# Where weights are split and which PSUM bank takes turned data: four edits to a two-layer trunk on one core

## The chip, the cores and the metric

One Trainium2 core runs the whole kernel. The metric is the device time of one execution in microseconds (us). TensorE is called PE, VectorE DVE, ScalarE ACT, GpSimd POOL. Each engine works through its own instruction order and waits for others by semaphores.

## The reference

The kernel computes a trunk of two layers over 256 latent tokens of width 1024 (with 256 context tokens that serve the first layer's keys and values). Layer 0 mixes by differential attention (six heads) and a Fourier part, layer 1 by a gated mixer (SGU). Each layer is followed by a product-key expert network (PEER) with 16384 experts, and a norm ends it. Everything is float32. Cut to the parts that the change touches:

```python
# layer 0: per head, probabilities from two softmaxes, then values
p = jax.nn.softmax(s, axis=-1)
a = p[:, :, 0] - lam * p[:, :, 1]
return jnp.einsum('bhqk,bkhe->bqhe', a.astype(v.dtype), v)
...
# layer 1: the gated mixer
z = jax.nn.gelu(h @ w_in + b_in)
u, v = jnp.split(z, 2, axis=-1)
v = rmsnorm(v, ng).reshape(B, L // CHUNK, CHUNK, SGU_GROUPS, SGU_GC)
s = jnp.einsum('gpq,bnqgc->bnpgc', ws, v) + bs.T[None, None, :, :, None]
return (u * s.reshape(B, L, SGU_W)) @ w_out
...
x = x + g1 * y
x = x + g2 * peer_mix(rmsnorm(x, norm2_g[i]) * (1 + sc2) + sh2, ...)
```

The gates g1, g2 and the scales come from one vector per layer (`c_s @ ada_w[i] + ada_b[i]`), which the kernel gathers in the background.

## The kernel before

**Split weights.** A float32 product is made of three faster ones: a weight tile `raw` (128 x 1024, half a megabyte, one column block of the output) is split into `whi` (rounded, by ACT, L108) and `wlo` (the rest, by DVE, L110), and an activation in the same way (`thi`/`tlo`, `mhi`/`mlo`, `m1hi`/`m1lo`). `lin` (L240) issues whi by hi, whi by lo, wlo by hi. `S.next()` hands out the next split weight and `S.ahead()` splits one more, if a buffer is free; where it stands in the program is where ACT and DVE do that work, since the kernel's order is written out by hand and nothing is moved afterwards.

**PSUM.** There are eight banks of 128 x 512 in three pools: `mm` (2), `gg` (2) and `acc` (4), handed out by `mmb()`, `gb()` and `accb()`. A new user of a bank waits until the old one's readers are done. `gg` serves sums of squares (L263), spreads of a factor over the partitions (L276), the rope's permutation (L709), and the gates' sum `Ada.cols` (L459).

**Mixer 0.** A loop over heads runs by the table HEADS. `scores_parts` (L723) writes four `acc` banks, DVE takes maxima (L725), ACT exponentials (L733); `blend` (L747) makes `aa`; `turn` transposes it by PE (L755) into two banks, which ACT copies to `aT` (L756); `values` (L763) multiplies. The table TAIL does the last heads, the Fourier part (L908, L912, L916) and the gates (`A`, which calls `ada.cols()`), and begins the output columns d=0 and 1 (`w`). Then the loop over d (L949) makes the other columns; `residual` (L496) adds each to `x` and, from d=2 on, splits the next weight.

**The seam into mixer 1.** After PEER 0, `tail` transposes the sum back (L1219) and adds it to x, two columns d in one bank. `Norm.products` then starts the mixer's products before the norm's factor is known: columns 0 and 1, the sum of squares (ACT squares, DVE adds into `acc`, L306; `total`, L263), column 2, `factor` (L276, after POOL's power on `ir`, L268) and so on. In this norm (`lag`) the squares are taken at j = 1.

**Mixer 1** runs by the table SGU. V0 to V7 are half products for v (L247 to L249), E adds the bias and takes the gelu (z, L1280, then ACT's vv and vn), r and m scale v (vn, L1294), U6, U7, G6 and G7 make the last of u. Then for each group k of 128: p multiplies by the spatial weights (PE, L1308), x makes s (DVE, L1314), m = s u (DVE, L1318) and m1hi (ACT, L1319), l makes m1lo (DVE, L1324), and w0k, w1k, w2k add it to three output columns (PE, L240) at once. S is `S.ahead()` and N opens the next norm. Columns 3 to 7 follow in a loop over d.

Of the kernel before, what the change touches and what calls it, by code (L numbers as in the profile page):

```python
# [53 lines left out]
TAIL = "F0 s0 s1 s2 F1 s3 F2 F3 s4 fc u3 S t4 A n3 d0 d1 b N S v4 c1 u4 t5 c0 w00 v5 w11 w12 u5 n4 w06 w01 w03 n5 w13 S w04 w07 w16 w14 w05 w02 w15 w10 w17".split()  # L54

N1 = 3
SGU = "V0 S V1 S R E0 E1 V2 S V3 S E2 E3 V4 S V5 S E4 E5 V6 S V7 S E6 E7 r m0 m1 U6 S G6 U7 S G7 N p0 x0 p1 x1 l0 p2 x2 l1 p3 x3 l2 w00 w10 w20 p4 x4 l3 w01 w11 w21 p5 x5 l4 w02 w12 w22 p6 x6 l5 w03 w13 w23 p7 x7 l6 w04 w14 w24 l7 S w05 w15 w25 w06 w16 w26 w07 w17 w27".split()
START = "Lc Lx M0 sc M1 M2 M3 M4 M5 sx ic ix b S M6 S rc nc2 nc1 nc0 rx nc6 nx1 nx2 nc3 M7 nx0 nx3 C0 S nx4 M8 S Dc0 M9 S Dx0 Q000 M10 nx5 S Q010 M11 nc4 M12 Q020 nx7 S nc5 M13 Q030 M14 nc7 M15 nx6 C1 Q100 S Lk Q110 Dx1 Dc1 a Q120 S Q021 Q130 Q121 Q001 S Q101 Q111 a S Q031 a a Q011 V0 Q131 a Q220 S Q200 a a Q230 Q210 Q221 a S Q201 V1 a S Q231 S Q211 a V2".split()
HEADS = "k sum a turn ks a S score a q a rk a kc qs exp blend a values rq sc norm a S".split()
ADA_AT = list(range(68, 116, 6)) + list(range(132, 190, 4)) + list(range(190, 256, 2))  # L60
# [102 lines left out]
def trunk(ctx, tc, a, out):  # L163
# [8 lines left out]
    def mmb():  # L172
        return ps.tile([P, 512], F32, name="mm", bufs=2)

    def gb():
        return ps.tile([P, 512], F32, name="gg", bufs=2)

    def accb():
        return ps.tile([P, 512], F32, name="acc", bufs=4)

    S = Stream(nc, raws, hls)
    seen = set()
    for s in START:
        if s[0] == "M":
            n = int(s[1:])
# [48 lines left out]
    def lin(p, unit, xhi, xlo, order=range(KT), first=True, last=True, n=T, passes=(0, 1, 2)):  # L234
        (whi, wlo), o = unit, p[:, :n]
        terms = (whi, xhi), (whi, xlo), (wlo, xhi)
        for j, k in enumerate(order):
            for i in passes:
                w, t = terms[i]
                nc.tensor.matmul(o, lhsT=w[:, k, :], rhs=t[:, k, :n], start=first and j == 0 and i == passes[0],  # L240
                                 stop=last and j == len(order) - 1 and i == passes[-1])
# [38 lines left out]
    class Norm:  # L280
# [33 lines left out]
        def products(self, n, evict):  # L314

            self.lows(KT)
            p, u, t = [], [], []
            S.held = 2
            for j in range(n):
                p.append(accb() if j < 4 else mmb())  # L320
                u.append(S.next())
                if 0 < j < n - 1:
                    S.ahead()
                if j == 1:
                    for k in range(KT if self.lag else 0):
                        self.square(k)
                    for k, i in ([(k, i) for k in range(KT) for i in range(2)] if self.lag else
                                 [(k, i) for i in range(2) for k in range(KT - 1)] + [(KT - 1, 0), (KT - 1, 1)]):
                        lin(p[i], u[i], thi, tlo, (k,), n=W, passes=(0, 2), first=k == 0, last=False)
                    if not self.lag:  # L330
                        self.total()
                    for i in range(2):
                        lin(p[i], u[i], thi, tlo, n=W, passes=(1,), first=False)
                    S.held = 1
                elif j > 1:
                    lin(p[j], u[j], thi, tlo, n=W)
                if j == 2 and self.lag:
                    self.total()
                if j == (3 if self.lag else 1):
                    self.factor()  # L340
                    t = [self.scaled(k) for k in range(4)]
                if j == 1:
                    S.ahead()
            t += [self.scaled(k) for k in range(4, 6)]
            early = 2 if self.lag else 0
            for i in range(early):
                self.evict(p, i, evict)
            for k in range(KT):
                sh = self.shift[:, k:k + 1]
                A_.activation(thi[:, k, :T], t[k], AF.Identity, bias=sh)  # L350
                V.scalar_tensor_tensor(tlo[:, k, :T], t[k], sh, thi[:, k, :T].bitcast(F32),  # L351
                                       op0=OP.add, op1=OP.subtract)
                if k + 6 < KT:
                    t.append(self.scaled(k + 6))
                if k == 4:
                    S.ahead()
            return lambda: [self.evict(p, i, evict) for i in range(early, n)]
# [136 lines left out]
    def residual(nrm, d, p, gate, ahead=False):  # L494
        def add():
            V.scalar_tensor_tensor(x[:, d, :], p, gate, x[:, d, :], op0=OP.mult, op1=OP.add)  # L496
        if ahead:
            S.ahead(add)
        else:
            add()  # L500
        nrm.feed(d)


    with ExitStack() as mx:
# [14 lines left out]
        with tc.tile_pool(name="m0n", bufs=2) as npl:  # L519
# [101 lines left out]
            for s in START:  # L621
                c, n = s[0], s[1:]
# [10 lines left out]
                elif c == "M":  # L633
                    n = int(n)
# [22 lines left out]
                elif c == "D":  # L657
                    h, j = int(n[1]), n[0]
# [91 lines left out]
        def turn(h):  # L750
            aT = tmp.tile([P, 4, T], F32, name="aT", bufs=1)
            for qt, aa in enumerate(ea.pop(h)):
                p = accb()
                for k in range(4):
                    nc.tensor.transpose(p[:, k * P:(k + 1) * P], aa[:, k * P:(k + 1) * P], ident)  # L755
                A_.activation(aT[:, :, qt * P:(qt + 1) * P], p.rearrange("p (k q) -> p k q", k=4), AF.Copy)  # L756
            av[h] = aT
# [108 lines left out]
        def tail_step(s):  # L866
# [13 lines left out]
            elif c == "t":  # L880
                assert isinstance(ea[n], list)
                turn(n)
            elif c == "v":
                values(n)
# [62 lines left out]
            tail_step(s)  # L947
        assert "N" in have
        S.held = 1  # L949
        for d in range(8):  # L950
            if d < 2:
                p, u = first[d]
            else:
                p = mmb()
                lin(p, S.next(), mhi, mlo)
            residual(nrm, d, p[:, :T], mod[:, 0, 16 + d:17 + d], d > 1)

    def peer(layer, nrm, ln, last):


        with ExitStack() as px:
# [111 lines left out]
            r = routing()  # L1073
            with tc.tile_pool(name="rq", bufs=2) as rq:
                for half in range(2):
# [5 lines left out]
                    for l in range(0 if half else LATE, 8):  # L1081
                        p = mmb()
# [9 lines left out]
                    for tt in range(2):  # L1092
                        for g in range(2):
                            p = accb()
# [4 lines left out]
                            l0 = half * 8 + g * 4  # L1099
# [45 lines left out]
            def y_mult(i, halves=range(2)):  # L1145

                w = thi[:, i % 8, :T], tlo[:, i % 8, :T]
                e = [u.rearrange("p k c -> p (k c)") for u in units[i]]
                for n, (a_, b_) in enumerate(((0, 0), (1, 0), (0, 1))):
                    for tt in range(2):  # L1150
                        for h in halves:
                            nc.tensor.matmul(y[2 * h + tt], lhsT=w[a_][:, tt * P:tt * P + P],  # L1152
                                             rhs=e[b_][:, 512 * h:512 * h + 512],
                                             start=i == 0 and n == 0, stop=i == 127 and n == 2)

            g0 = gphase(0)
            for i in range(128):
# [6 lines left out]
                p = accb() if i < 120 else mmb()  # L1164
# [35 lines left out]
            def tail(ys):  # L1200

                ys = [t.rearrange("p (t c) -> p t c", t=2) for t in ys]
                for h in range(2):
                    if h == 0:
                        for i in range(128 - last, 128):
                            y_mult(i, (0,))
                    else:
                        y_mult(127, (1,))
                    A_.activation(ys[h][:, 0], y[2 * h], AF.Copy)
                    V.tensor_copy(ys[h][:, 1], y[2 * h + 1])  # L1210
                    if h == 0:
                        for i in range(128 - last, 127):
                            y_mult(i, (1,))
                    for d in range(4 * h, 4 * h + 4):
                        if d % 2 == 0:
                            p = mmb()
                        q = p[:, d % 2 * T:d % 2 * T + T]
                        for tt in range(2):
                            nc.tensor.transpose(q[:, tt * P:tt * P + P], ys[h][:, tt, d % 4 * P:d % 4 * P + P], ident)  # L1219
                        yield d, q, mod[:, layer, 40 + d:41 + d]  # L1220
# [7 lines left out]
    with mixer1 as mx:  # L1228
# [111 lines left out]

        for s in SGU:
            step1(s)
        assert "N" in have and wdone == [8] * N1
        S.held = 1
        for d in range(8):
            if d < N1:
                p = first[d][0]
            else:
                p = mmb()
# [127 lines left out]
```

## Time and profile before

| what | us |
| --- | --- |
| median of 3 runs | 1989.8 |
| lowest, highest | 1985.33, 1990.18 |
| the profiled execution's own time | 1987.19 |
| its span on the core | 1985.0 |
| PE busy in it | 1930.5 |
| DVE busy in it | 1567.0 |
| ACT busy in it | 935.9 |

Times in the rows below count from the start of the span. In the timeline a row merges instructions of one kind that follow one another; the number behind the x says how many. The idle time ahead of an instruction and who ended it stand in brackets. PE's idle time over the whole span is 54.5 us. The granted clock of PE is 1.00 (2.4 GHz) or 0.50 (1.2 GHz); its mean was 0.992.

### The profile page before, as it was taken

What the parts mean: (1) busy time and instruction counts of PE and PEld (TensorE: products, weight loads), DVE (VectorE), ACT (ScalarE), POOL (GpSimd) and SP (SyncE); (2) the same over time, 40 slices, a digit from 0 to 9 for tenths busy, and PEclk for the clock granted to TensorE, in tenths of its full rate; (3) what the DMA queues carried; (4) which work ended last, traced back from release to release, by engine and by line L of the source; (5) the groups of instructions that cost most, each with busy time, mean ns of one, the idle gap of its engine ahead of it and who ended that gap; (6) DMA issues with size and microseconds to landing.
All of it is one profiled execution on the core that took longest, in us unless ns stands there. A gap on an engine that the chain in (4) does not pass through costs nothing. (4 is left out here: it accounts for less than half of the span.)

```text
span 1985.0 us, 35614 instructions
## 1 busy us (share of the span) xinstructions
PE 1930.5 (97%) x14176; PEld 1726.4 (87%) x14176; DVE 1567.0 (79%) x2978; ACT 935.9 (47%) x1489; POOL 11.1 (1%) x17
## 2 busy tenths in 40 slices
PE   7999999999999999999998899999999999999997
PEld 3977999999999877788888899999999977778885
DVE  5786789987887899998887778997777788885554
ACT  5445554454444444444446554445444444444443
POOL 0000000000000000000000000000000000000000
PEclk8999999999999999999999999999999999999998
DMA  7742556656665566688885455555555555556662
GB/s 267 268 165 72 170 170 184 188 175 199 190 191 180 185 209 197 202 260 280 282 285 173 137 183 171 188 184 181 170 167 164 170 165 173 162 180 186 187 189 74
DMA packets 106150, 373.50 MB, mean 188 GB/s; under 512 B 11904, under 2 KB 12544, under 8 KB 105600
## 3 DMA queue, kind: packets, MB, share of 16 engines
q1 hardware_dynamic: 104256, 366.23, 57.6%
q10 hardware_dynamic: 1728, 5.00, 0.8%
q8 instruction: 111, 1.82, 0.4%
q14 instruction: 55, 0.45, 0.1%
HBM read 370.14 MB, written 1.05 MB: 187 GB/s over the span
## 5 line engine op out<-in xcount | busy, mean ns | idle before, releaser
L110 DVE TENSOR_TENSOR wlo<-raw,whi 128x1024 fp32r<-128x1024 f32 x604 | 737.3, 1223 | 225.1 <-ACT whi L108 217.1
L108 ACT ACTIVATE whi<-raw 128x1024 fp32r<-128x1024 f32 x604 | 635.5, 1055 | 418.2 <-PE acc L1152 328.1
L240 PE MATMUL acc<-thi,whi 128*128 128x256 f32 (+1 forms) x2016 | 571.1, 284 | 0.0
L240 PE MATMUL acc<-thi,wlo 128*128 128x256 f32 (+1 forms) x2016 | 567.7, 282 | 0.4 <-DVE wlo L110 0.4
L240 PE MATMUL acc<-tlo,whi 128*128 128x256 f32 (+1 forms) x2016 | 560.0, 281 | 0.0
L240 PEld LDWEIGHTS acc<-thi,wlo 128*128 128x128 f32 x2016 | 381.9, 189 | 1.0 <-DVE wlo L110 0.8
L240 PEld LDWEIGHTS acc<-thi,whi 128*128 128x128 f32 x2016 | 381.1, 189 | 0.0
L240 PEld LDWEIGHTS acc<-tlo,whi 128*128 128x128 f32 x2016 | 376.4, 188 | 0.0
L1152 PE MATMUL acc<-whi,thi 128*128 128x512 f32 x1024 | 285.6, 400 | 0.0
L1152 PE MATMUL acc<-whi,tlo 128*128 128x512 f32 x1024 | 281.3, 396 | 0.0
L1152 PE MATMUL acc<-wlo,thi 128*128 128x512 f32 x1024 | 281.1, 395 | 0.0
L1173 ACT ACTIVATE A<-acc 128x256 f32<-128x256 f32 x240 | 92.5, 386 | 394.0 <-PE acc L240 394.0
L1152 PEld LDWEIGHTS acc<-wlo,thi 128*128 128x128 f32 x1024 | 192.6, 188 | 47.5
L1152 PEld LDWEIGHTS acc<-whi,tlo 128*128 128x128 f32 x1024 | 192.6, 188 | 44.9
L1152 PEld LDWEIGHTS acc<-whi,thi 128*128 128x128 f32 x1024 | 187.2, 188 | 39.3
L1138 DVE SCALAR_TENSOR_TENSOR A<-gg,A 128x512 f32<-128x512 f32 x128 | 88.4, 690 | 74.8 <-PE gg L1135 74.8
L240 PE MATMUL mm<-thi,whi 128*128 128x256 f32 (+1 forms) x448 | 128.6, 287 | 0.9 <-ACT qp L1089 0.9
L240 PE MATMUL mm<-tlo,whi 128*128 128x256 f32 (+1 forms) x448 | 127.0, 284 | 2.4 <-DVE tlo L351 2.4
L240 PE MATMUL mm<-thi,wlo 128*128 128x256 f32 (+1 forms) x448 | 126.4, 282 | 0.0
L492 DVE TENSOR_TENSOR tlo<-A,thi 128x256 fp32r<-128x256 f32 x256 | 107.3, 420 | 0.0
L491 ACT ACTIVATE thi<-A 128x256 fp32r<-128x256 f32 x256 | 102.5, 401 | 0.0
L1135 PEld LDWEIGHTS <-o 128*128 128x128 f16 x2048 | 69.7, 97 | 31.3 <-DVE og L1124 13.5
(265 smaller groups left out, 2013.3 us busy)
## 6 DMA issues: line engine op xcount, KB each, us to landing
raw<-in_eu SPq DMA_DIRECT2D x256, 512.0 KB, 3.6
raw<-in_ev SPq DMA_DIRECT2D x256, 512.0 KB, 4.2
raw<-in_ada1t SPq DMA_DIRECT2D x56, 512.0 KB, 4.5
raw<-in_wq SPq DMA_DIRECT2D x32, 512.0 KB, 4.2
ada<-in_ada0t SPq DMA_DIRECT2D x48, 256.0 KB, 5.1
raw<-in_ada0h SPq DMA_DIRECT2D x16, 512.0 KB, 4.8
raw<-in_w_out SPq DMA_DIRECT2D x16, 512.0 KB, 3.7
raw<-in_o_in_u SPq DMA_DIRECT2D x8, 512.0 KB, 5.1
```

What stands on the lines that cost most here:

```text
L108: nc.scalar.activation(hi, r, AF.Copy)
L110: nc.vector.tensor_tensor(lo, r, hi.bitcast(F32), op=OP.subtract)
L240: nc.tensor.matmul(o, lhsT=w[:, k, :], rhs=t[:, k, :n], start=first and j == 0 and i == passes[0], stop=last and j == len(order) - 1 and i ...
L491: A_.activation(hi, src, AF.Copy)
L492: V.tensor_tensor(lo, src, hi.bitcast(F32), op=OP.subtract)
L1135: nc.tensor.matmul(pt[:, t, :], lhsT=o2[:, t // 2, :, t % 2], rhs=og[j][:, t // 2, :, t % 2], start=j == 0, stop=j == 1)
L1138: V.scalar_tensor_tensor(av, pt.rearrange("p t i -> p i t"), 1.0 / GSCALE, av, op0=OP.mult, op1=OP.mult)
L1152: nc.tensor.matmul(y[2 * h + tt], lhsT=w[a_][:, tt * P:tt * P + P], rhs=e[b_][:, 512 * h:512 * h + 512], start=i == 0 and n == 0, stop=i = ...
L1173: A_.activation(A[i // 64][:, i % 64, :], p[:, :T], AF.Gelu_apprx_tanh)
```

## The change

It has four parts. (1) `turn` takes its two banks from `gg`, not `acc`. (2) One more `S.ahead()` stands ahead of mixer 0's loop over d. (3) At the seam into mixer 1 the squares stand ahead of the splits, and `tail` takes every second bank from `gg`. (4) The table SGU has its S in other places.

```diff
-SGU = "V0 S V1 S R E0 E1 V2 S V3 S E2 E3 V4 S V5 S E4 E5 V6 S V7 S E6 E7 r m0 m1 U6 S G6 U7 S G7 N p0 x0 p1 x1 l0 p2 x2 l1 p3 x3 l2 w00 w10 w20 p4 x4 l3 w01 w11 w21 p5 x5 l4 w02 w12 w22 p6 x6 l5 w03 w13 w23 p7 x7 l6 w04 w14 w24 l7 S w05 w15 w25 w06 w16 w26 w07 w17 w27".split()
+SGU = "V0 S V1 S R E0 E1 V2 S S V3 S E2 E3 V4 S S V5 S E4 E5 V6 S V7 E6 E7 r m0 m1 U6 U7 G6 G7 p0 x0 p1 x1 l0 p2 x2 l1 p3 x3 l2 w00 w10 w20 p4 x4 l3 w01 w11 w21 N p5 x5 l4 S w02 w12 w22 p6 x6 l5 w03 w13 w23 p7 x7 l6 S w04 w14 w24 l7 w05 w15 w25 w06 w16 w26 w07 w17 w27 S".split()
...
-                if 0 < j < n - 1:
+                if 0 < j < n - 1 and not (self.lag and j == 1):
                     S.ahead()
                 if j == 1:
                     for k in range(KT if self.lag else 0):
                         self.square(k)
+                    if self.lag:
+                        S.ahead()
...
             for qt, aa in enumerate(ea.pop(h)):
-                p = accb()
+                p = gb()
...
         S.held = 1
+        S.ahead()
         for d in range(8):
...
                         if d % 2 == 0:
-                            p = mmb()
+                            p = gb() if d % 4 else mmb()
```

Three places show how it moves the instructions. A row is one engine's instruction (or several alike) in program order: line, operation, output and inputs, shape. The change's lines are 2 to 3 higher than the same lines before.

**PE in mixer 0's tail.** `ones` and `osq` are a head's sum of squares, `ident` and `aa` the transposes of `turn` for head 4, `blocks` and `fold` the gates' sum. Before:

```order
L263 MATMUL acc<-ones,osq 128x1 x2
L755 MATMUL acc<-ident,aa 128x128 x8
L459 MATMUL gg<-blocks,fold 128x24 x4
L276 MATMUL acc<-ident,ir 128x128 x2
L908 MATMUL mm<-cst,ft 128x512 x4
L763 MATMUL acc<-aT,vt 128x256 x4
```

With the change:

```order
L263 MATMUL acc<-ones,osq 128x1 x2
L757 MATMUL gg<-ident,aa 128x128 x8
L461 MATMUL gg<-blocks,fold 128x24 x4
L276 MATMUL acc<-ident,ir 128x128 x2
L910 MATMUL mm<-cst,ft 128x512 x4
L765 MATMUL acc<-aT,vt 128x256 x4
```

The order is the same; the eight transposes now fill both gg banks (four each), and the gates' sum takes one of the two right after them.

**DVE at the seam into mixer 1.** `tlo` are the low parts of x, `acc` the sum of squares, `ir` the sum's first step after L263, `nt` the normed x. Before:

```order
L310 SCALAR_TENSOR_TENSOR tlo<-x,sc_81,thi 128x256 x8
L110 TENSOR_TENSOR wlo<-raw,whi 128x1024 x2
L306 TENSOR_TENSOR acc<-acc,sq 128x256 x7
L110 TENSOR_TENSOR wlo<-raw,whi 128x1024 x2
L268 TENSOR_SCALAR ir<-gg 128x2
L110 TENSOR_TENSOR wlo<-raw,whi 128x1024
```

With the change:

```order
L310 SCALAR_TENSOR_TENSOR tlo<-x,sc_81,thi 128x256 x8
L306 TENSOR_TENSOR acc<-acc,sq 128x256 x7
L110 TENSOR_TENSOR wlo<-raw,whi 128x1024 x4
L268 TENSOR_SCALAR ir<-gg 128x2
L110 TENSOR_TENSOR wlo<-raw,whi 128x1024
```

The two splits whose first weight serves column 2 moved behind the seven additions; on ACT their two whi moved behind the eight squares in the same way.

**DVE in the gated mixer, from vn on.** s, m and m1lo are the steps x and l of the table. Before, from vn to the first rounds:

```order
L1294 TENSOR_SCALAR vn<-vv,rv 128x1024
L110 TENSOR_TENSOR wlo<-raw,whi 128x1024 x2
L289 TENSOR_TENSOR tlo<-mod,thi 128x8x2
L1314 SCALAR_TENSOR_TENSOR s<-acc,cols,bsb 128x256
L1318 TENSOR_TENSOR m<-s,ut 128x256
```

and its end (x6 to the first residual):

```order
L1314 SCALAR_TENSOR_TENSOR s<-acc,cols,bsb 128x256
L1318 TENSOR_TENSOR m<-s,ut 128x256
L1324 TENSOR_TENSOR m1lo<-m,m1hi 128x256 x2
L110 TENSOR_TENSOR wlo<-raw,whi 128x1024 x2
L496 SCALAR_TENSOR_TENSOR x<-mm,mod,x 128x256
```

With the change, from l2 to the first residual:

```order
L1327 TENSOR_TENSOR m1lo<-m,m1hi 128x256
L110 TENSOR_TENSOR wlo<-raw,whi 128x1024 x2
...
L1327 TENSOR_TENSOR m1lo<-m,m1hi 128x256
L110 TENSOR_TENSOR wlo<-raw,whi 128x1024
...
L1321 TENSOR_TENSOR m<-s,ut 128x256
L1327 TENSOR_TENSOR m1lo<-m,m1hi 128x256
L110 TENSOR_TENSOR wlo<-raw,whi 128x1024
L1327 TENSOR_TENSOR m1lo<-m,m1hi 128x256
L110 TENSOR_TENSOR wlo<-raw,whi 128x1024
L498 SCALAR_TENSOR_TENSOR x<-mm,mod,x 128x256
```

The two wlo between vn and the first s are gone; s0 follows vn directly. Two wlo now stand behind l2 (the first of them is the weight of output column 2, which w20 needs), one behind l4, one between l6 and l7, and one between l7 and the residual. On ACT each of their whi stands behind the m1hi of the x step ahead of it. In the V phase the three groups of wlo between the z steps are 2, 2 and 2 before, and 3, 3 and 1 with the change.

## Rows read from the trace of the kernel before

**Rows 1.** The page: busy time, share of the span and instructions by engine.
```profile
PE 1930.5 (97%) x14176; PEld 1726.4 (87%) x14176; DVE 1567.0 (79%) x2978; ACT 935.9 (47%) x1489; POOL 11.1 (1%) x17
```

**Rows 2.** Timeline, 172 to 184: start, length, engine, line, operation, [idle before, releaser].
```profile
172.32 1.14 PE L723 MATMUL acc<-kh,qh 64*128 64x512 f32 x4 [1.09 <-DVE qh L712]
...
180.21 1.07 PE L755 MATMUL acc<-ident,aa 128*128 128x128 f32 x8
...
181.06 2.02 ACT L108 ACTIVATE whi<-raw 128x1024 fp32r<-128x1024 f32 x2
181.11 0.97 PE L459 MATMUL gg<-blocks,fold 128*128 128x24 f32 x8
...
182.95 1.10 ACT L756 ACTIVATE aT<-acc 128x512 f32<-128x512 f32 x2
```

**Rows 3.** Timeline, 198 to 206, PE and DVE.
```profile
199.00 0.28 PE L240 MATMUL mm<-mlo,whi 128*128 128x256 f32 x1
...
199.99 0.48 DVE L496 SCALAR_TENSOR_TENSOR x<-mm,mod,x 128x256 f32<-128x256 f32 x1
...
205.43 0.39 PE L240 MATMUL mm<-mhi,wlo 128*128 128x256 f32 x1 [1.15 <-DVE wlo L110]
```

**Rows 4.** Timeline of the seam, 1056 to 1071, PE and DVE.
```profile
1056.76 3.25 DVE L310 SCALAR_TENSOR_TENSOR tlo<-x,sc,thi 128x256 fp32r<-128x256 f32 x8
...
1061.92 0.28 PE L240 MATMUL acc<-thi,whi 128*128 128x258 f32 x1
...
1062.20 3.60 DVE L306 TENSOR_TENSOR acc<-acc,sq 128x256 f32<-128x256 f32 x7
...
1065.85 0.61 PE L263 MATMUL gg<-ones,acc 128*128 128x1 f32 x4 [0.91 <-DVE acc L306]
...
1068.44 0.15 DVE L268 TENSOR_SCALAR ir<-gg 128x2 f32<-128x2 f32 x1
...
1070.33 0.71 PE L276 MATMUL gg<-ident,ir 128*128 128x128 f32 x4 [0.90 <-POOL ir L269]
```

**Rows 5.** Timeline of the V phase, DVE and ACT.
```profile
1089.65 1.99 ACT L108 ACTIVATE whi<-raw 128x1024 fp32r<-128x1024 f32 x2
...
1090.73 2.36 DVE L110 TENSOR_TENSOR wlo<-raw,whi 128x1024 fp32r<-128x1024 f32 x2 [2.55 <-ACT whi L108]
...
1093.01 0.75 DVE L1280 TENSOR_TENSOR z<-acc,bvb 128x256 f32<-128x256 f32 x2
```

**Rows 6.** Timeline from p0 to the end of l2.
```profile
1108.38 2.22 PE L1308 MATMUL acc<-wsT,vn 128*128 128x128 f32 x16 [1.50 <-DVE vn L1294]
...
1112.23 0.48 DVE L1314 SCALAR_TENSOR_TENSOR s<-acc,cols,bsb 128x256 f32<-128x256 f32 x1
...
1113.21 0.42 ACT L1319 ACTIVATE m1hi<-m 128x256 fp32r<-128x256 f32 x1 [1.76 <-DVE m L1318]
...
1113.68 0.39 PE L240 MATMUL mm<-m1hi,whi 128*128 128x256 f32 x1 [3.08 <-ACT m1hi L1319]
...
1116.33 0.42 DVE L1324 TENSOR_TENSOR m1lo<-m,m1hi 128x256 fp32r<-128x256 f32 x1
```

**Rows 7.** Groups by line, 1056 to 1128: count, busy, mean ns, idle before and releaser.
```profile
L110 DVE TENSOR_TENSOR wlo<-raw,whi 128x1024 fp32r<-128x1024 f32 x19 | 22.6, 1221 | 9.9 <-ACT whi L108 9.8
L108 ACT ACTIVATE whi<-raw 128x1024 fp32r<-128x1024 f32 x19 | 19.1, 1043 | 0.0
```

**Rows 8.** Timeline, 1119 to 1128, DVE and PE.
```profile
1119.05 0.48 DVE L1314 SCALAR_TENSOR_TENSOR s<-acc,cols,bsb 128x256 f32<-128x256 f32 x1 [1.12 <-PE acc L1308]
...
1123.06 0.99 DVE L1324 TENSOR_TENSOR m1lo<-m,m1hi 128x256 fp32r<-128x256 f32 x2
...
1127.48 0.36 PE L240 MATMUL mm<-m1hi,whi 128*128 128x256 f32 x1 [1.08 <-DVE x L496]
```

**Rows 9.** Windows, TensorE: length, busy (instructions), granted clock, DMA share, GB/s.
```profile
1108.38:1110.60 2.22, 2.22 (x16) 1.00 0.01 4
...
1115.78:1119.19 3.41, 3.41 (x18) 0.50 0.04 16
```

## The prediction

> **What bounds the kernel now.** I read the page first: TensorE (PE) is busy 1930.5 us of the span, 97% [rows 1], so only its 54.5 us of idle time can be won, and anything that makes PE wait longer is lost in full. Then I read the program order of before and of the change beside each other, and the timeline at each place that the change touches, to see what ends PE's wait there. The places are the tail of the first mixer (180 to 206 us), the seam into the second mixer (1056 to 1078) and the gated mixer (1077 to 1130). Outside them PE is back to back and the order is the same.
>
> The sum is made against the profiled execution, 1987.19 us with a span of 1985.0; the median of the runs shown is 1989.8, 2.6 us above it. One part in 0.3% is 6 us, about what a measurement of this kernel can tell from no change.
>
> **Turned probabilities in the gates' banks.** In the heads loop scores no longer share banks with `turn`. PE waits there for `qh` at the head's end, which VectorE (DVE) sets: the last head's scores wait 1.09 us for it [rows 2], and DVE does the same work as before, so what the scores win inside a head is given back there. I take 0; bounds +0.3 (the second half of `turn` now waits for the rope's `rm`) and -1.4.
>
> The tail pays. Before, `turn` of head 4 (L755) ran at 180.21 to 181.28 and the gates' sum (L459) followed at 181.11 without a wait [rows 2]. Now both halves of `turn` take the two gg banks, and L459 needs one of them, so it waits until ScalarE (ACT) has copied the first `aT` out. ACT gets to that at 182.95, since two splits whi that start at 181.06 stand ahead; the pair takes 1.10, so the first is out at about 183.55 and L459 starts at 183.65. That is **+2.55**. Queued behind L459 on PE are the spread L276, the Fourier products L908 and the values L763; ACT's fx waits for L908, so its later work slides as well. Bounds +1.5 (some of it caught up where PE waits later) to +2.6.
>
> **One split ahead of the d loop.** PE's wait of 1.15 us for wlo at 205.43 goes [rows 3]. But the moved wlo now stands ahead of x0 on DVE. Its whi must wait for the buffer that d=0's last product with whi frees (the row at 199.00, done 199.29); whi 1.04 gives 200.36, the next DVE instruction can start 1.14 after wlo's start at 200.39, so x0 runs at 201.53 and not at 199.99. d=2's product needs x0's bank: it starts at 202.15 and not at 200.61, 1.54 later. **+0.1** net as the two cancel (1.54 against 1.15 and the short waits around it); bounds -0.4 and +0.4.
>
> **Squares ahead of splits.** The wait of 0.91 us at 1065.85 for the sum of squares goes [rows 4]. The eight tlo end at 1060.01, the seven additions take 3.60, so `acc` is complete at 63.5 instead of 65.8. But the third product's weights are split only after the squares: ACT's last square is done 0.6 before the last addition, at about 62.9, whi at 63.9, wlo at 65.1. That product began at 1061.92; now its first two matmuls run at 63.9 and the third waits until 65.15, where it would have been at 62.2. So it ends 2.9 later, the sums come 2.9 - 0.91 = 2.0 later, and the next product too. The spread L276 waited 0.90 for POOL's ir; ir itself comes at 1068.44 as before, since four wlo in a row reach to 68.5. So 2.0 - 0.9 and rounding leave the spread at 1071.2 to 1071.4: **+0.9**; bounds +0.5 and +1.3.
>
> **Seam transposes in gg.** The wait on DVE's x is between the two halves of one bank and stays, so 0; bounds -0.3 and +0.3.
>
> **The gated mixer's table.** Four steps.
> 1. In the V phase z, ACT's vv and vn, whi, wlo and the next z form one chain: whi 1089.65, wlo 1090.73, the next z 1093.01 [rows 5]. Each wlo adds 1.14 (two take 2.36). Before the last z there were six wlo in three groups of two, now there are 3 + 3 + 1. So vn and p0 come 1.14 later; with the seam's 0.9, p0 starts at 1108.38 + 2.04 = 1110.42.
> 2. Before, two wlo and a tlo stood between p0 and the first s, which ran at 1112.23 though p0 was done about 0.9 after its start [rows 6]. Now s0 follows p0 at 1111.35. From s0 to the end of l2 before took 1112.23 to 1116.75, 4.52; so l2 ends at 1115.87, and x3's m1hi (0.42, behind x3's m) at 1115.99.
> 3. Only then are the weights of the third output column (w2) split: whi 1.04 to 1116.95 and wlo 1.22 to 1118.2 [rows 6, 7]. PE has w00 and w10 done by 1114.2, stops 2.9 us for whi and 1.0 for wlo. A second wlo runs to 1119.34, s4 at 1119.25. Then two further splits stand inside the chain, after l4 and after l6, and each whi waits on ACT for the m1hi ahead of it. By the same durations: s5 1120.88, l4 1121.74, wlo 1123.26 to 1124.49, s6 1124.40, two rounds of s, m, l, m1hi of x7 1127.0, whi 1127.94, wlo 1129.2. l7 stands behind that wlo and ends at 1129.53, where before it ended at 1124.05 [rows 8].
> 4. A last split (the S at the table's end) stands ahead of x0. Its whi waits for w07's second product with whi, about 1130.0; whi 1131.0, wlo 1131.06, x0 1132.2 to 1132.7, and d=3, which needs x0's bank, starts at 1132.83 and not at 1127.48: 5.35 later, of which 0.9 is the seam's. The table: **+4.45**. After that PE is dense as before.
> Bounds of the table: +2 (if whi of w2 slips in between m1hi) and +6.
>
> Sum at full clock: 2.55 + 0.1 + 0.9 + 4.45 = +8.0.
>
> **The clock.** After PE's wait of 3.08 us (1110.60 to 1113.68) the granted clock was 0.50 from 1115.78 to 1119.19 [rows 6, 9]; after the single wait of 1.50 that ends at 1108.38 it stayed 1.00. The new waits (2.5 at L459, 1.8 and 1.0 at the seam, 2.6 at p0, 2.9 and 1.0 at w2, 2.3 at d=3) lie between and above. Where PE sets the pace, 3.41 us at half clock lose 1.7; in the w stretch DVE lost 1.12 waiting for p5 [rows 8]. I count one such stretch in the w stretch and two more of the three other places: 1.1 + 1.7 + 1.7 = **+4.5**; bounds 0 and +7. The old one at 1115.78 isn't subtracted: its cost does not enter the new chain, which I built from DVE and ACT rows.
>
> The Trainium skill ("TensorE: Matmul & The Clock Gate", Terms) puts the penalty at the throttled time times what the gate takes away, half here. The row of 1115.78 shows less, 1.12, as PE partly waited for DVE anyway; by the page three stretches would cost 5.1 and the sum would be 13.1.
>
> Total +12.5: 1987.2 + 12.5 = 1999.7. I say 2000.
>
> **The rivals.**
> - *Stalls without the clock.* The new waits fall so that the clock stays up, or its losses hide behind DVE: +8.0, 1995 (1997.8 from the median). For it: 3.41 us is short, and two waits of 2.5 may be split by work. Against: 3.9 us of waits lie nearly together at w2.
> - *The splits slip in, not slower.* Place: whi of w2 on ACT. m1hi of x0 to x3 leaves ACT free 0.8 us in each round. It decides if whi is done before m1hi of x1; it would take a different order of ACT's queue than the table writes, or s0 so early that the m1hi are through by 1112. Then w00 would start at 1112.9 against 1113.68 with no stop at w2, the l chain would end 1 us ahead of before, and d=3 would start within 1 us of 1127.5: table -1, total 2.55 + 0.1 + 0.9 - 1 = +2.5, 1990. Against it: the m1hi are ahead of whi in the order.
> - *Heads win.* Scores that start early let the head's DVE work start early: three heads of 0.5 us, -1.4, and the last score of the tail earlier. Alone it would not turn the sign. With the rival above it ends at 1988.
> - *The change doesn't do what it says.* "Further ahead" is true of the V phase only; w2's weights are split later than before (after x3 instead of at p0). If the order shown were not what runs, nothing would change: 1987 to 1990.
>
> **How the numbers follow.** Forecast (stalls and some clock) 0.55, stalls alone 0.22, splits slip in 0.12, heads with it 0.05, no effect 0.06. Slower by over 0.3%: all of the first bar a tenth, and three quarters of the second, where +8 less the bounds of the small terms comes under 6: 0.50 + 0.17 = 0.67 and some of the third, 0.69. Within 0.3%: 0.25. Faster: 0.06. The range goes from stalls alone with the lower bounds, +4.5, to all clock losses and the upper ends, +18, and takes in that the runs of before spread from 1985.3 to 1990.2: 1991 to 2006.
>
> **What would show it.** Right: L459 with a wait of some 2.5 us released by aT; the third product of the seam waiting for whi, then wlo, and no wait left at L263; PE stopped at acc<-m1hi,whi in the w stretch; l7 behind a wlo; d=3 released by x some 5 us later against p0's neighbours; granted clock 0.50 in at least one place more than before. Wrong: w20 without a wait, or x0 within 1.5 us of the last w; a tail whose L459 follows at once.

## The result, and the profile after

The changed kernel takes 2001.73 us (median of 6 runs, 1999.08 to 2004.77) against 1988.44 us for the kernel before (6 runs, 1985.33 to 1990.18): a ratio of 1.0071, 95% interval 1.0057 to 1.0084, so slower by about 13 us. Its profiled execution took 2000.82 us with a span of 1998.6, that is 13.6 us more span than before. The numbers of lines are 2 higher than before up to the seam and 3 higher in the gated mixer.

The first fence is the page of the changed kernel: busy time, share of the span and instructions by engine.

```profile
PE 1936.2 (97%) x14176; PEld 1731.3 (87%) x14176; DVE 1566.9 (78%) x2978; ACT 937.2 (47%) x1489; POOL 10.3 (1%) x17
```

DVE and ACT do the work that they did in [rows 1]. PE runs the same 14176 matmuls but is busy for 5.7 us more, so the loss is waiting and slower matmuls together: 13.6 - 5.7 = 7.9 us are PE's idle time and 5.7 us matmuls that took longer. Both are sums over the whole span, places that gain included. That 7.9 lies near the stalls of the prediction's sum (8.0) proves nothing; the table below goes by place.

The timeline of the tail, 178 to 186 (columns as in [rows 2]):

```profile
179.43 1.07 PE L757 MATMUL gg<-ident,aa 128*128 128x128 f32 x8
...
180.28 2.02 ACT L108 ACTIVATE whi<-raw 128x1024 fp32r<-128x1024 f32 x2
...
182.17 1.10 ACT L758 ACTIVATE aT<-gg 128x512 f32<-128x512 f32 x2
...
182.84 1.90 PE L461 MATMUL gg<-blocks,fold 128*128 128x24 f32 x8 [2.34 <-ACT aT L758]
```

In [rows 2] the gates' sum followed `turn` without a wait. Now PE stands 2.34 us ahead of it, until the first `aT` is out, which ACT makes behind two whi. Then the sum takes 1.90 us and not 0.97, at half clock (the windows below). The d loop, 204 to 240, the only PE wait over 1 us in it:

```profile
207.04 0.35 PE L240 MATMUL mm<-mhi,whi 128*128 128x256 f32 x1 [1.70 <-DVE x L498]
```

The wait of 1.15 us for wlo [rows 3] has turned into one for x. The seam, 1060 to 1078, PE, ACT and DVE:

```profile
1064.49 3.59 DVE L306 TENSOR_TENSOR acc<-acc,sq 128x256 f32<-128x256 f32 x7
...
1067.38 2.94 ACT L108 ACTIVATE whi<-raw 128x1024 fp32r<-128x1024 f32 x3
...
1068.48 0.39 PE L240 MATMUL acc<-thi,whi 128*128 128x258 f32 x1 [1.83 <-ACT whi L108]
...
1069.74 0.58 PE L240 MATMUL acc<-thi,wlo 128*128 128x258 f32 x1 [0.76 <-DVE wlo L110]
...
1073.98 0.50 PE L263 MATMUL gg<-ones,acc 128*128 128x1 f32 x4
...
1077.30 0.61 PE L276 MATMUL gg<-ident,ir 128*128 128x128 f32 x4
```

The waits for the sum and for `ir` [rows 4] are gone; the third product waits for whi and then wlo in their place, both standing behind ACT's last square. The gated mixer, every PE wait over 0.3 us from p0 to d=3:

```profile
1116.38 3.13 PE L1311 MATMUL acc<-wsT,vn 128*128 128x128 f32 x16 [2.61 <-DVE vn L1297]
...
1122.93 0.38 PE L240 MATMUL acc<-m1hi,whi 128*128 128x256 f32 x1 [2.00 <-ACT whi L108]
...
1124.19 0.49 PE L240 MATMUL acc<-m1hi,wlo 128*128 128x256 f32 x1 [0.76 <-DVE wlo L110]
...
1132.98 0.39 PE L240 MATMUL mm<-m1lo,whi 128*128 128x256 f32 x1 [0.70 <-DVE m1lo L1327]
...
1136.83 0.39 PE L240 MATMUL mm<-m1lo,whi 128*128 128x256 f32 x1 [1.33 <-DVE m1lo L1327]
...
1140.02 0.39 PE L240 MATMUL mm<-m1hi,whi 128*128 128x256 f32 x1 [1.98 <-DVE x L498]
```

And what DVE and ACT did there, the four places of the table's steps 2 to 4:

```profile
1117.30 0.48 DVE L1317 SCALAR_TENSOR_TENSOR s<-acc,cols,bsb 128x256 f32<-128x256 f32 x1 [0.97 <-PE acc L1311]
...
1121.51 0.42 ACT L1322 ACTIVATE m1hi<-m 128x256 fp32r<-128x256 f32 x1 [0.77 <-DVE m L1321]
1121.84 1.99 ACT L108 ACTIVATE whi<-raw 128x1024 fp32r<-128x1024 f32 x2
...
1135.21 1.23 DVE L110 TENSOR_TENSOR wlo<-raw,whi 128x1024 fp32r<-128x1024 f32 x1 [1.10 <-ACT whi L108]
1136.36 0.42 DVE L1327 TENSOR_TENSOR m1lo<-m,m1hi 128x256 fp32r<-128x256 f32 x1
1138.34 1.23 DVE L110 TENSOR_TENSOR wlo<-raw,whi 128x1024 fp32r<-128x1024 f32 x1 [1.57 <-ACT whi L108]
1139.48 0.48 DVE L498 SCALAR_TENSOR_TENSOR x<-mm,mod,x 128x256 f32<-128x256 f32 x1
```

The weights of w2 are split only once x3's m1hi has left ACT, the last m1lo runs right behind a wlo, and x0 right behind another. Windows of PE at the four places (columns as in [rows 9]), from the tail and from the seam to d=3:

```profile
182.24:189.06 6.82, 6.22 (x17) 0.50 0.48 154
```

```profile
1069.70:1073.11 3.41, 3.37 (x15) 0.50 0.68 178
1117.49:1120.90 3.41, 3.41 (x16) 0.50 0.00 0
1124.32:1127.73 3.41, 3.41 (x17) 0.50 0.74 201
1141.38:1144.79 3.41, 3.41 (x18) 0.50 0.26 103
```

Between 150 and 1960 us the kernel before had one stretch at half clock, 3.41 us long [rows 9]. Now there are five, 20.5 us together, and each begins during one of the waits shown or within 1.4 us of its end.

Both traces hold the same matmuls in the same order, so each can be set against its own. The same stretch of program in both, place by place (after less before, us; one trace of each kernel):

| place | forecast at full clock | measured | of it more than the stall |
| --- | --- | --- | --- |
| start to the last head's scores (172) | 0 | -0.78 | |
| tail, to the second sum of squares (194.11; before 189.26) | +2.55 | +5.63 | 3.12 |
| d loop and the rest up to the seam | +0.1 | -0.29 | |
| seam | +0.9 | +2.34 | 1.56 |
| V phase, to p0 | +1.14 | +1.10 | |
| p0 to d=3 (1140.02; before 1127.48) | +3.31 | +4.54 | 1.23 |
| d=3 to the end | 0 | +1.06 | 1.06 |
| sum | +8.0 | +13.6 | 6.97 |

In the tail the stall is the later start of the gates' sum, 182.84 against 181.11 with the 0.78 added back, 2.51. At the seam it is PE's idle time, 1.83 + 0.76 against 0.91 + 0.90, 0.78. From p0 on it is the forecast from DVE and ACT rows, which the instructions met up to the end of l2 (below). Of the 1.06 behind d=3, 1.0 is there 3.6 us later, in the last stretch at half clock.

### The profile page after: what moved, and what is told of

Read it like the earlier page. It is cut to its first block, busy times and chain, and to the rows that moved or that the text cites. A ratio compares the mean times of both kernels' runs of the same rounds, so it can differ in the third digit from the quotient of the medians.

```text
span 1998.6 us, 35615 instructions
## 1 busy us (share of the span) xinstructions
PE 1936.2 (97%) x14176; PEld 1731.3 (87%) x14176; DVE 1566.9 (78%) x2978; ACT 937.2 (47%) x1489; POOL 10.3 (1%) x17
## 3 DMA queue, kind: packets, MB, share of 16 engines
HBM read 370.14 MB, written 1.05 MB: 186 GB/s over the span
```

## The experiments

The theory: wherever a part of the change makes ACT or DVE do other work ahead of what PE needs next, PE waits for the time worked out, and behind the longer waits the clock is half for a time. The first rival: the stalls alone, without the clock. The second: one part carries it all and the others are free.

### One part at a time

**The banks of `turn` alone** (a1_turn).

```diff
-                p = accb()
+                p = gb()
```

> The kernel before with one edit: turn takes its two banks from gg. My account (a new wait of L459, then half clock): +5.6 us of PE time between 172 and 195 us of the span, of which 2.5 are the wait at L459 for the first aT and 3.1 two stretches at half clock behind it; the whole kernel 1988.4 + 5.6 = 1994. Rival (the wait alone, the clock stays up without the other edits): +2.5, 1991. Rival (scores win in the heads what the tail loses): 1988 to 1989, with the head loop at least 1 us shorter.

1992.43 us against 1989.31, ratio 1.0017 (1.0007 to 1.0026). The wait ahead of the gates' sum is as in the full change. One stretch at half clock follows it, where two were expected, and the time is 1.6 us under the 1994 expected. Its timeline of PE, then its window:

```profile
183.88 1.07 PE L459 MATMUL gg<-blocks,fold 128*128 128x24 f32 x8 [2.35 <-ACT aT L756]
```

```profile
185.77:189.18 3.41, 3.41 (x6) 0.50 0.68 243
```

From the last head's scores to the second sum of squares it takes 21.23 us (172.59 to 193.82), 4.29 more than before: 2.50 of stall and 1.8 of clock.

**The squares ahead of the splits alone** (a2_seam): in `products`, the hunk with `self.square(k)` of the change, nothing else.

> The kernel before with one edit: at the seam the squares stand ahead of both splits of j = 1. My account: column 2 waits about 1.8 us for whi and 0.8 to 1.1 for wlo, the waits of 0.91 (sums) and 0.90 (ir) go, net +0.9 at full clock and +2.3 with a stretch at half clock; the kernel 1989.3 to 1990.7. Rival (the squares win 0.9 to 1.8 as their waits go): 1987.

1990.29 us, ratio 1.0012 (1.0003 to 1.0022). The seam shows the waits of the full change to 0.02 us:

```profile
1064.11 0.39 PE L240 MATMUL acc<-thi,whi 128*128 128x258 f32 x1 [1.84 <-ACT whi L108]
...
1065.37 0.58 PE L240 MATMUL acc<-thi,wlo 128*128 128x258 f32 x1 [0.75 <-DVE wlo L110]
```

A stretch of 3.41 us at half clock begins at 1064.89, and the products behind the seam come about 2.1 us later against its start: 0.78 of idle time, 1.3 of clock.

**The gated mixer's table alone** (a3_table): the new line `SGU`, nothing else.

> The kernel before with one edit: the table SGU of the change. My account: p0 1.1 us later, the third output column waits for its whi and wlo (2.8 us together), l7 and x0 stand behind a wlo, d=3 starts about 5.6 later, and half clock at d=3 brings that to 6.8; the kernel 1995. Rival (the table is harmless and the tail carries the loss): within 2 us of 1988.4.

1997.22 us, ratio 1.0042 (1.0026 to 1.0059), the largest part. The waits of p0, of w2 for whi and wlo, and of d=3:

```profile
1111.94 2.22 PE L1308 MATMUL acc<-wsT,vn 128*128 128x128 f32 x16 [2.62 <-DVE vn L1294]
...
1118.49 0.58 PE L240 MATMUL acc<-m1hi,whi 128*128 128x256 f32 x1 [2.58 <-ACT whi L108]
...
1119.75 0.58 PE L240 MATMUL acc<-m1hi,wlo 128*128 128x256 f32 x1 [0.46 <-DVE wlo L110]
...
1135.88 0.58 PE L240 MATMUL mm<-m1hi,whi 128*128 128x256 f32 x1 [1.98 <-DVE x L496]
```

Two stretches of 6.83 us at half clock begin at 1117.67 and 1134.74. In this trace the gated mixer loses 8.0 us from the start of the V phase, 1.2 more than the 6.8 expected and 1.3 more than in the changed kernel; the stretch at d=3 is twice as long here.

**The two small parts** (a4_small): one `S.ahead()` ahead of the d loop, and the seam's transposes in `gg`.

```diff
         S.held = 1
+        S.ahead()
...
-                            p = mmb()
+                            p = gb() if d % 4 else mmb()
```

> The kernel before with the two small edits: one more split ahead of mixer 0's d loop, and every second seam bank from gg. My account: PE's wait of 1.15 us for wlo turns into one of 1.7 for x0's bank, net -0.2 to +0.1; the seam's waits of 0.58 and 0.75 stay; the kernel 1988.4 within 1. Rival (a split further ahead pays in full): -1.15, and -2.6 more if the seam's waits go.

1989.58 us, ratio 1.0000 (0.9991 to 1.0010). d=2 waits 1.70 for x in place of the 1.15 for wlo and the short waits around it: nothing won, nothing lost.

The four differences add up to 0.17 + 0.12 + 0.42 + 0.00 = 0.71%, the ratio of the whole change. That they meet it to the digit is chance, as each is known to 0.1 or 0.2 only. The table carries over half, but three of the four cost something, so the second rival falls.

### Taking one suspected wait away

**The gates' sum in a bank of another pool** (b1_cols): the changed kernel, where `cols` of the tail takes an `acc` bank.

```diff
-        def cols(self):
+        def cols(self, bank=gb):
...
-            p = gb()
+            p = bank()
...
-                ada.cols()
+                ada.cols(accb)
```

> The changed kernel with one edit: the gates' sum in mixer 0's tail takes a bank of acc, turn keeps gg. My account (the wait is for the bank): L459 (L461 in the change) follows the transposes within 0.3 us, the wait of 2.34 and the half clock behind it go, -3 to -5.6: 1996 to 1998.5. Rival (the tail is late for another cause, ACT's queue or the spread): the time stays within 1 us of 2001.7.

1996.34 us, ratio to the kernel before 1.0041 (1.0027 to 1.0055), 5.4 us less than the changed kernel. The wait at L461 is gone, and with it the half clock there:

```profile
181.31 0.97 PE L461 MATMUL acc<-blocks,fold 128*128 128x24 f32 x8
```

From the last scores to the second sum of squares it takes 16.93 us, as before (16.94). The wait for a bank is thus shown to be the cause of the tail's whole loss in the trace.

**Dummy products ahead of the gates' sum** (b5_fill): nine 128 x 128 products that no one reads, to keep PE at work where it waits.

```diff
+                fill = mmb()
+                for _ in range(9):
+                    nc.tensor.matmul(fill[:, :P], lhsT=ident, rhs=ident, start=True, stop=True)
                 ada.cols()
```

> The changed kernel with nine 128x128 products more (into an mm bank, read by nobody) ahead of the gates' sum in mixer 0's tail: about 2.4 us of work in the place of the 2.34 us wait. My account (half of the tail's loss is the clock): L461 runs at the same place within 0.3 us, the granted clock stays 1.00 through 182 to 189, and PE reaches the head's sum (L263 after L765) 1.7 to 3.1 us earlier than in the changed kernel: 1998.6 to 2000. Rival (the clock costs nothing here, the later work waits for ACT and DVE anyway): no change in the tail, 2001.7.

In place the clock part went away. The window that stood at 0.50 in the changed kernel, of this one (its tail runs some 2 us later, and the clock stays at 1.00 to 1068 us):

```profile
182.24:189.06 6.82, 6.49 (x41) 1.00 0.44 133
```

From the first to the second sum of squares it took 12.02 us (181.21 to 193.23), where the kernel before took 9.4 and the changed one 15.0: the stall stays and the 3 us behind it go. But the whole is no shorter, against 1998.6 to 2000 expected: 2002.17 us, ratio 1.0067 (1.0051 to 1.0084). In its trace the stretches at half clock at the seam and at d=3 are 6.83 us long (1068.25 and 1139.93), twice those of the changed kernel, and two are new (3.41 us at 143.24 and 173.96). What moved them isn't settled by this run.

**The table's first half alone** (d1_pairs): the kernel before, with the V phase's splits in groups of 3 + 3 + 1 and none behind U6.

```diff
- ... V2 S V3 S E2 E3 V4 S V5 S E4 E5 V6 S V7 S E6 E7 r m0 m1 U6 S G6 U7 S G7 N ...
+ ... V2 S S V3 S E2 E3 V4 S S V5 S E4 E5 V6 S V7 E6 E7 r m0 m1 U6 G6 U7 S G7 N ...
```

> The kernel before with the changed table's first half alone: the splits of the V phase in groups of 3 + 3 + 1 and none behind U6, from the groups' start (p0) on everything as before. It tells step 1 of the table (p0 comes 1.1 us later) from steps 3 and 4 (the third column's splits and the two in the chain). Theory: p0 waits 2.6 instead of 1.5 us, but one wlo fewer (1.14) stands between p0 and the first s, so the first m1hi comes when it did, the wait of 3.08 us there shrinks to about 2, and no loss is left: 0 to +0.6 us, 1989 to 1989.6, ratio 0.9998 to 1.0003; the table's +8 then lies in steps 3 and 4 alone. Rival (p0's delay is lost in full, with a half-clock stretch behind the longer wait): +1.1 to +2.8 us, ratio 1.0006 to 1.0014.

1987.33 us against 1988.19, ratio 0.9994 (0.9985 to 1.0003): the theory, not the rival. p0 waits as in the full change, and the wait of 3.08 us for m1hi [rows 6] shrinks:

```profile
1110.36 3.68 PE L1308 MATMUL acc<-wsT,vn 128*128 128x128 f32 x16 [2.61 <-DVE vn L1294]
1114.70 0.39 PE L240 MATMUL mm<-m1hi,whi 128*128 128x256 f32 x1 [0.67 <-ACT m1hi L1319]
```

Measured against the start of the V phase (0.85 us later here than before), p0 comes 1.13 later, the first w 0.17 later and d=3 1.40 earlier. The clock fell to half at 1110.38, during p itself, and the first w still came only 0.17 later. So the later p0 is paid back, and the table's loss lies in the splits that stand behind it: those of w2, and those in and behind the chain.

### The same means put elsewhere

**Another table** (b2_table): the kernel before with no split of the table between p0 and l7. `Q` does r between the whi and the wlo of one split; `Y` is a split for which one buffer is left.

```diff
- ... E0 E1 V2 S V3 S E2 E3 V4 S V5 S E4 E5 V6 S V7 S E6 E7 r m0 m1 U6 S G6 U7 S G7 N p0 ... l7 S w05 ...
+ ... E0 E1 S V2 V3 E2 E3 S S V4 V5 E4 E5 S S V6 S V7 E6 E7 Q m0 m1 S U6 U7 G6 G7 p0 ... w21 N p5 ... l7 Y w05 ...
+            elif c == "Q":
+                S.ahead(lambda: step1("r"))
+            elif c == "Y":
+                held, S.held = S.held, MIX_BUFS - 1
+                S.ahead()
+                S.held = held
...
-            residual(nrm, d, p[:, :T], mod[:, 1, 16 + d:17 + d], d >= N1)
+            residual(nrm, d, p[:, :T], mod[:, 1, 16 + d:17 + d], d == 0 or d >= N1)
```

> The kernel before with another table SGU: the E steps stand ahead of the splits that follow V3, V5 and V6, one split is ahead of E6's z instead of two, one goes between r and m0, one (not two) between vn and s0, none inside the x and l rounds, one (not two) ahead of the first residual and one behind it. My account (z chain, wlo ahead of s0 and x0): z6 about 2.4 us earlier, p0 right after U7 (1.5 gained), s0 3.8 earlier, d=3 5 to 6 earlier: 1983 to 1984.5. Rival (DVE's total work sets the stretch, not the places of the splits): within 1 us of before.

1984.86 us, ratio 0.9982 (0.9972 to 0.9991): faster. p0 waits 1.29 and the first w 1.00 us, PE is at full clock from there to d=3, and d=3 has no wait (the column behind it waits 0.57 for its wlo). Against the start of the V phase p0 comes 0.85 us later and d=3 4.1 earlier, where 1.5 earlier and 5 to 6 earlier were expected. One thing that it still pays stands in the V phase, a wlo that is late for V6:

```profile
1098.74 0.39 PE L248 MATMUL acc<-wlo,thi 128*128 128x256 f32 x1 [0.77 <-DVE wlo L110]
```

**The d loop's split one column earlier** (b4_dloop): the kernel before, with a split around d=1's addition to x (whi, the addition, wlo); the change had put one ahead of the loop.

```diff
-            residual(nrm, d, p[:, :T], mod[:, 0, 16 + d:17 + d], d > 1)
+            residual(nrm, d, p[:, :T], mod[:, 0, 16 + d:17 + d], d > 0)
```

> The kernel before with one edit: in mixer 0's d loop the split that serves d=3 is issued around the residual of d=1 (whi, then x1, then wlo), so it is not ahead of x0. My account: the wait of 1.15 for wlo at d=3 goes and x0 is not late: -1.1, 1987 to 1988.3. Rival (ACT's whi ahead of the thi of d=1 delays the norm): 0.

The wait of 1.15 us [rows 3] is gone and none took its place; from the last scores to the loop's end it is 1.7 us shorter in the trace. The times can't tell it: 1988.25 us against 1988.87, ratio 0.9999 (0.9990 to 1.0009).

**The sum ahead of one split at the seam** (b3_seam): only at j = 2, and no squares moved.

```diff
-                if 0 < j < n - 1:
+                late = self.lag and j == 2
+                if 0 < j < n - 1 and not late:
                     S.ahead()
...
-                if j == 2 and self.lag:
+                if late:
...
+                    S.ahead()
```

> The kernel before with one edit: at the seam the third product's adding of squares to the sum comes ahead of that product's split instead of behind it; the splits for the other products stay as they are. Theory (the change's loss at the seam lies in the second product's split, which it moved behind the squares, not in the sum's order): the wait of 0.9 us for the sum of squares goes or shrinks, the third product's weights are in time, nothing is lost: -0.5 to -0.9 us in the trace, 1988 to 1989, ratio 0.9995 to 1.0. Rival (any split behind the sum makes a product late): a wait of about 1 us for a split weight at the next product, so 0 to +2 us, ratio 1.000 to 1.001.

The wait for `ir` went, that for the sum stayed at 0.91:

```profile
1065.36 0.61 PE L263 MATMUL gg<-ones,acc 128*128 128x1 f32 x4 [0.91 <-DVE acc L306]
...
1068.79 0.63 PE L276 MATMUL gg<-ident,ir 128*128 128x128 f32 x4
```

The spread comes 1.05 us earlier against the seam's start, and no product became late. I had the right size with the wrong wait. The times can't tell a microsecond: 1987.96 us against 1989.01, ratio 0.9997 (0.9988 to 1.0006).

**The three together** (c1_all): the edits of b2_table, b4_dloop and b3_seam.

> The kernel before with the three edits that take waits away: the gated mixer's table with the splits between heads of work in the order that was tried alone (-4 us), the residual of the first mixer's second product ahead of its split (-1.7 in the trace), and the sum of squares ahead of the third product's split at the seam (-0.5 to -0.9). Theory (waits add, each gone wait gives back its length and the half-clock stretch behind it): -5.5 to -7 us, 1982 to 1984, ratio 0.9967 (0.996 to 0.9975). Rival (a gone wait comes back at the next place, or the half-clock stretches move): only the table's -3.6, ratio 0.998.

1982.96 us against 1989.01, ratio 0.9972 (0.9960 to 0.9983): some 6 us faster than the kernel before, as expected. The interval doesn't part it from the rival's 0.998. In the trace each edit gives its part in place: 1.7 us in the d loop, 1.05 at the seam, 3.6 in the gated mixer, where PE is at full clock from 1108 to 1134. But 2.3 us are lost between 150 and 172 us, around a stretch at half clock at 160.11 that no edit is near.

**The same with the V phase's pairs of splits parted** (c2_vphase): the table reads `E0 E1 S V2 V3 S E2 E3 S V4 V5 S E4 E5 S V6 S V7 E6 E7 Q`.

> The same as the kernel with the three edits, but in the gated mixer's first phase each pair of splits is parted: one ahead of the E steps, one behind. Theory (the chain z, vv and vn, whi, wlo, next z grows by 1.14 us with each wlo that stands ahead of z, and the first product's weight was late by 0.8 there): the 0.8 us wait goes, and 0 to 1 us more is won against the other kernel: 1981.5 to 1984, ratio 0.9962 to 0.9973. Rival (the parted splits make each z late instead): the first product of the gates starts later by about 1 us and nothing is won, ratio 0.997 to 0.998.

1984.13 us, ratio 0.9979 (0.9970 to 0.9988), so not shown to be better than the one before it. The V phase's wait of 0.77 is gone, but vn comes later, and PE is slower behind it:

```profile
1108.76 2.73 PE L1316 MATMUL acc<-wsT,vn 128*128 128x128 f32 x16 [2.33 <-DVE vn L1302]
```

This is the rival: PE waits 1 us more at p0 (2.33 against 1.29 in c1_all); with it a stretch of 6.83 us at half clock is back at 1109.95.

## Why the prediction was right, point by point

The kernel became slower, by the mechanism forecast, and 2001.73 lies 1.7 us from the 2000 said. The stalls came out as worked out; the clock was the term that was mis-sized. That the total is so near is luck in part: in the two traces the clock cost 2.5 us more than forecast and all else 1.4 less, of which 0.78 was gained before 172 us, mostly ahead of every edit. The range was no tight test either, and its lower end, +4.5, is not what the lower bounds add up to (+1.9).

- **Turned probabilities in the gates' banks.** 0 in the heads: up to 172 us the changed kernel is 0.78 ahead, but 0.65 of it is there by 30 us and 0.76 by 91 us, ahead of the first `turn` (101.21), so the heads won nothing. In the tail the stall was 2.51 for 2.55, and giving the gates' sum another bank took the whole of the tail's loss away (b1_cols).
- **One split ahead of the d loop.** +0.1 forecast, -0.16 measured in the loop itself, inside its bounds.
- **Squares ahead of splits.** +0.9 forecast, 0.78 of idle time measured, with the waits where they were put: less the 4.56 us by which the seam starts later, the third product's first matmul waiting for whi runs at 1063.92 and that waiting for wlo at 1065.18, where 63.9 and 65.15 were forecast. The wait on `ir` went as the sum assumed, but the way there was wrong. `ir` was to come at 1068.44 as before, with the spread at 1071.2 to 1071.4. PE ran at half clock from 1069.70, so the sum of squares came 3.6 later and not 2.0; DVE waited 1.43 for it, `ir` came at 1069.96 (1074.52 less 4.56) and the spread at 1072.74.
- **Seam transposes in gg.** 0, as far as a4_small tells.
- **The gated mixer's table.** p0 to the first s: 0.93 forecast, 0.92 measured. From that s to the end of l2 4.52, both. whi of w2 stands behind x3's m1hi as said, 1121.84. PE's waits for it were 2.00 and 0.76, not 2.9 and 1.0: w00 and w10 ran at half clock and ended later, so less was left to wait. x0 was forecast 21.8 us behind p0 and came 23.1 behind it. The excess of 1.3 is all there at s5: DVE waited 0.30 for p4 and 0.85 for p5, with PE at half clock from 1124.32 to 1127.73; from s5 to x0 the forecast holds. Step 1's +1.14 was met too, but is not a loss by itself (d1_pairs): steps 3 and 4 carry the table.
- **The clock.** The term that was off: +4.5 forecast, its upper bound +7, about 7.0 in the one pair of traces (what is left when the stalls are taken off). I counted two of the three places tail, seam and d=3, at 1.7 each, and one in the w stretch at 1.1. All four had one, the tail's was twice as long (6.83 us, 3.1 lost), the seam's cost 1.56, the w stretch 1.23 and d=3 1.06. The Trainium skill ("TensorE: Matmul & The Clock Gate", Terms) would give half of the 17.1 us that stand at half clock more than before, 8.5. The trace gives 7.0, and the measurement decides: the slow products from 1117.49 to 1120.90 stand ahead of a wait for whi that they only made shorter. In the old stretch at 1115.78 too PE was busy throughout [rows 9], so it was not, as I wrote, a wait of PE within it that made it cheap.
- **The rivals.** Stalls without the clock falls by the windows at 0.50, and in the tail by b5_fill, where 3 us went in place with the clock at 1.00. The splits slipping in falls by ACT's order, m1hi at 1121.51, then whi at 1121.84. That the heads win falls with the first point above, and that nothing changes by the times.

What stays open is the clock's price as a whole. The banks of `turn` cost 3.1 us alone and 5.4 within the change, with the same wait of 2.3 us; the intervals overlap, but in the traces one stretch of 3.41 us follows that wait alone and one of 6.83 within the change. Filling the wait won nothing in total. Nor is the price the program's alone. Over the recorded runs of the kernel before, the span and the mean granted clock go together, from 1983.2 us at 0.994 to 1989.8 at 0.989, with no edit at all. So the 7.0 holds for the one pair of traces, and another pair could show another figure. What sets where a stretch falls, and how long it is, no run here isolates.

## What to carry to other kernels

Where an engine's order is written by hand, "ahead" means ahead of what stands behind it on that engine: ask for each moved split what it now delays, and put it where that work has slack (the V phase, not the w chain). A bank pool that a rare user shares is worth a look when another user moves in, since the rare one waits for a reader on a third engine. When PE bounds the kernel, price a new wait at its length, and the half clock that may follow it as a range of its own. Here it was nothing behind the 1.70 us in the d loop, and 1.1 to 3.1 us behind the waits at d=3, the seam and the tail (1.98, 1.83 + 0.76 and 2.34 us).

## What the runs showed of the hardware

Between the start and about 1965 us the half clock came in stretches of 3.41, 6.83 and 10.24 us; each trace has one longer stretch, of 15.6 to 18.8 us, at its end. It also came where no edit was near. Three kernels (a3_table, b2_table, d1_pairs) run the program of the kernel before up to the V phase, and have 6.83 us at half clock near 141 us, where the kernel before has 3.41 at 105.43; two of the three have 3.41 more at 568. The kernel with the three edits has 6.83 us at 160.11, inside heads that it runs like the kernel before. The same wait did not bring the same clock. Ahead of p0 PE stood 2.6 to 3.0 us in five traces, and its first sixteen products then took 2.22 us (the table alone, 2.62; the dummy products, 2.98), 3.13 (the changed kernel, 2.61), 3.33 (the gates' sum in another pool, 2.63) and 3.68 (the table's first half, 2.61); after 1.29 us they took 2.05. So the length of a wait did not tell in these runs whether, or where, the clock would fall.
